# The opening of a decoder layer: c spread over partitions by TensorE, a plain second gate, and eight modulation columns computed later

## The chip, the cores and the metric

The kernel runs on one core of a Trainium2 chip. The metric is the device time of one execution in microseconds. A core has a matrix engine (TensorE, PE in the profile), which loads a stationary operand (PEld) and streams a moving one past it, and three others for elementwise work: VectorE (DVE), ScalarE (ACT) and GpSimd (POOL). SyncE (SP) issues the DMAs here. Data stands in SBUF, 128 partitions wide; matmul results stand in PSUM, in eight banks of 128 x 512 f32.

## The reference

One decoder layer on x (1024 tokens x 1024) with a condition c (one row of 1024):

```
mods = SiLU(c) @ W_ada + b_ada            # 9 rows of 1024: shift, scale, gate of 3 sub-layers
x = LN1(alpha*x + (1+g1) * 1/2 * SwiGLU_1(x*(1+sc1) + sh1))
x = LN2(alpha*x + (1+g2) * TokenMix(x*(1+sc2) + sh2))
x = LN3(alpha*x + (1+g3) * 1/2 * SwiGLU_2(x*(1+sc3) + sh3))
SwiGLU(h) = (silu(h @ w_gate) * (h @ w_up)) @ w_down      # w_gate, w_up: 1024 x 2816
```

TokenMix is two groups of attention heads between an input and an output projection; the change does not touch it. All inputs are f32.

## The kernel before

**Exact products.** Every f32 operand of a large matmul is split in a high part (ACT casts it to fp32r, line 101) and a low part (DVE subtracts, line 102). `mm3` then issues three matmuls, high x high, high x low and low x high (lines 106 to 108), into one PSUM bank.

**Modulation.** A column block of 128 modulation values is the dot product of 128 rows of the transposed W_ada (`adaT`) with SiLU(c). SiLU(c) stands as a row on every partition (`silu`, 128 x 1024). `ada_mul` (line 119) multiplies one 128 x 1024 block by it and sums along the row, on DVE; the bias comes in as the start value of the sum, and the columns of `modc` take the results. There are 72 such blocks: 16 for shift and scale of the first FFN (m = 0, 1), computed in the opening, and 56 others. `more_ada` (line 655) issues these one by one beside FFN 1: each combination step of a product calls it through `beside`, it adds 57 to a count, and whenever the count reaches 120 it takes the next block of `rest`: a DMA into ring `q` and one `ada_mul` on DVE behind that combination step.

**FFN, gate and up.** The 22 column tiles of 128 of w_gate and w_up are worked in 11 groups of two. A group's gate, and then its up part, is a 2 x 2 block product (two weight column tiles by two token halves of 512, over two halves of the 1024 rows). From group 1 on it is done with seven block products instead of eight (class `Seven`, after Winograd): each is 4 x 3 = 12 matmuls, 84 in all, against 96 for the plain form. For this, `w_ops` (line 246) combines weight blocks on DVE (lines 265 to 271) and splits seven of them; the moving side takes the blocks B11, B21, B22 of the modulated input and the combinations T1 to T4 (`t_sum`, line 219; `t_split`, line 238); and the products are combined out of PSUM on DVE (lines 306 to 327). `use_gate` then forms gate * (1 + tanh(gate/2)) and `use_up` multiplies by the up part. `a_store` writes the group's result with its own combinations to DRAM for the down projection.

**Opening.** Lines 530 to 538 load c twice, each half spread by a DMA to all 128 partitions, and form SiLU(c). `start_ffn1` (line 562) works group 0 in the plain form, in eight chunks of 128 rows of x, `d` = 0 to 7: load two blocks of adaT and one of x^T, compute the two modulation columns, modulate (ACT, line 598), split, and issue 24 matmuls into eight PSUM banks (weights `w0` and `w1`, each a gate and an up tile). From d = 4 on each chunk also forms T1 to T4 of rows d - 4 and splits T1 and T2. Then come SiLU and product of group 0 (lines 627 to 629), the weights of group 1's gate (line 630) and the splits of T3 and T4.

**FFN 2** uses the same code. Its first three pairs of products are begun early, while the second token half is still being normalized (line 1306); two of these keep their sums in ring `b` until lines 308 to 313 and 341 or 345 have read them. After that `gate_up` runs at line 1330, and `more_ada` with it (line 1329), with nothing left in `rest`.

**Buffers and order.** Tiles come from rings (line 41): `h` 14 of 8 KB per partition, `w` 6, `u` 6, `t` 7, `z` and `q` 4, `b` 2. PSUM banks have rings too: `mm` 3, `y` 2, `tp` 2, `o` 1. A tile waits until a buffer of its ring is free. The order of instructions on each engine is laid out by the framework's planner, from its own estimate of when operands and buffers are ready, and can differ from the order of the code; on the chip each engine then works its list in order.

Of the kernel before, what the change touches and what calls it, by code (L numbers as in the profile page):

```python
# [9 lines left out]
AF = mybir.ActivationFunctionType  # L10
# [4 lines left out]
P = 128  # L15
# [30 lines left out]
def layer_kernel(ctx, tc, xT, x, c, adaT, adab, wg1, wu1, wd1, wqk, wv1, wv2, bf, sinks,  # L46
# [26 lines left out]
    def psum(tag):  # L73
        return mk(ps, [P, HT], F32, tag, BANK[tag])
# [39 lines left out]

        return [st("h", [P, 4, HT], F32R) for _ in range(2)]

    silu = st("b", [P, D])

    def ada_mul(w, j):
        m = j // KD  # L120
        s = 0.125 if m in (2, 8) else 0.5
        V.tensor_tensor_reduce(w, w, silu, scale=s, scalar=bcol[:, j:j + 1], op0=ALU.mult,
                               op1=ALU.add, accum_out=modc[:, j:j + 1])

    def ada_block(m, d):
# [162 lines left out]
    class Seven:  # L288


        def __init__(self, ops, use):
            self.ops, self.use, self.n, self.wo = ops, use, 0, {}

        def run(self, order, hold=None):
            for i in order:
# [52 lines left out]
    def gate_up(wg, wu, ops, ai, g0, wo, a=None, begun=()):  # L348
        ahead = list(begun)

        def order_of(s):
            return ORDER0 if s.n else ORDER

        def go(s):
            if s.n:
                s.use(0, 0, s.c11)
            s.run(order_of(s))

        for g in range(g0, NG):
            prev = a  # L360
            a, sg, su = ahead.pop(0) if ahead else gu_pair(ops)
            sg.wo.update(wo)
            su.wo.update(w_ops(wu, 2 * g, order_of(su)))
            go(sg)
            if prev:
                a_store(ai, g - 1, prev)
            wo = w_ops(wg, 2 * g + 2, order_of(ahead[0][1]) if ahead else ORDER) if g + 1 < NG else None
            go(su)
        a_store(ai, NG - 1, a)
# [157 lines left out]
        return xs[1]  # L527


    for n in range(2):  # L530
        cs = slice(n * HT, (n + 1) * HT)
        DMA.dma_start(silu[:, cs], c[0, cs].partition_broadcast(P))
        th = st("t", [P, HT])
        A.activation(th, silu[:, cs], AF.Tanh, scale=0.5)
        V.scalar_tensor_tensor(silu[:, cs], th, 1.0, silu[:, cs], op0=ALU.add, op1=ALU.mult)
    DMA.dma_start(bcol, adab)
    for m in (1, 4, 7, 2, 5, 8):
# [24 lines left out]
    def start_ffn1():  # L562
        ops = {}
        hd = []
        blk = {}
        w0 = w1 = None
        p0 = [[psum("mm"), psum("mm")], [psum("mm"), psum("o")]]
        p1 = [[psum("y"), psum("y")], [psum("tp"), psum("tp")]]
        ada = {}

        def fetch(d):
            if d < KD:
                ada[d] = st("h", [P, 2, D])
                for m in range(2):
                    j = m * KD + d
                    DMA.dma_start(ada[d][:, m], adaT[j * P:(j + 1) * P, :])
                hd.append(st("z" if d < 4 else "q", [P, S]))
                DMA.dma_start(hd[d], xT[d * P:(d + 1) * P, :])

        def modulation(d):  # L580
            if d < KD:
                for m in range(2):
                    ada_mul(ada[d][:, m], m * KD + d)

        fetch(0)
        modulation(0)
        for d in range(KD):
            t = hd[d]
            if d:
                fetch(d + 1)  # L590
            if d in (0, SECOND):
                if d == 0:
                    w0 = [weight_std(wg1, 0, "w"), weight_std(wu1, 0, "w")]
                for _, load in w0:
                    load(d > 0)
            if d == 0:
                fetch(1)
            A.activation(t, t, AF.Identity, bias=modc[:, d:d + 1], scale=modc[:, KD + d:KD + d + 1])
# [12 lines left out]
            for w, p in ((w0, p0), (w1, p1)):  # L611
                for q in range(2):
                    for hf in range(2):
                        hi, lo = blk[d // 4, hf]
                        mm3(p[q][hf], *w[q][0][d], hi[:, d % 4], lo[:, d % 4], d == 0, d == KD - 1)
            if d >= 4:
                for n in ("T1", "T2", "T3", "T4"):
                    t_sum(n, hd, ops, d - 4, V)
                for n in ("T1", "T2"):
                    t_split(n, ops, d - 4)  # L620
        ops["B11"], ops["B21"], ops["B22"] = blk[0, 0], blk[1, 0], blk[1, 1]
        a = []
        for j, p in enumerate((p0, p1)):
            a.append(st("z", [P, S]))
            for hf in range(2):
                t = halves(a[j])[hf]
                A.activation(t, p[0][hf], AF.Tanh, scale=0.5)
                V.scalar_tensor_tensor(t, t, 1.0, p[0][hf], op0=ALU.add, op1=ALU.mult)
                V.tensor_tensor(t, t, p[1][hf], ALU.mult)
# [4 lines left out]
        return ops, wo, a  # L634

    ops1, wo1, a1 = start_ffn1()

    DMA.dma_start(ident, consts[0])
    DMA.dma_start(upper, consts[1])
# [5 lines left out]
    V.memset(ones, 1.0)  # L645
    V.memset(nhalf, -0.5)
    V.tensor_scalar(nsink, sinkb, -1.0, None, op0=ALU.mult)

    rest = [(m, d) for m in range(2, 9) for d in range(KD)]

    rows_due = []

    pace = [0, 0]

    def more_ada(after, every):


        pace[0] += every
        if pace[0] < 120:
            return  # L660
        pace[0] -= 120
        while rows_due:
            gate_store(*rows_due.pop(0))
        if rest:
            m, d = rest.pop(0)
            with tc.issue_after(after):
                ada_block(m, d)
            if d == KD - 1 and m in (2, 5, 8):
                rows_due.append(((2, 5, 8).index(m), m))
# [9 lines left out]
    last_rows()  # L679

    xpark = [dram([S, D], f"xpark{i}") for i in range(2)]

# [777 lines left out]
```

## Time and profile before

| | us |
|---|---|
| median of 3 runs | 1785.83 |
| lowest and highest | 1784.86, 1786.31 |
| the profiled execution | 1786.12 |
| its span | 1784.3 |

Of the span, PE is busy 1742.3 (98%), DVE 1511.6 (85%), ACT 781.1 (44%), POOL 23.7 (1%). Busy times of DVE and ACT count overlapping starts and ends, so operations that follow one another closely show a little more each than their distance.

A row of the timeline gives start, length, engine, line, operation, output and inputs with their shapes, how many instructions were merged, and in brackets how long the engine had been idle before it and what released it. In the views by window, each engine has its busy time and the number of instructions.

### The profile page before, as it was taken

The page shows a single profiled execution, that of the slowest core. Times are in us where ns is not written, and L with a number is a line of the kernel's source. Part 1 is how long each engine was busy: PE and PEld are TensorE (multiplying, and loading weights), DVE is VectorE, ACT ScalarE, POOL GpSimd, SP SyncE. Part 2 cuts the span into 40 slices and gives each one's busy share as a digit, 9 for nine tenths or more (in the row PEclk, how much of TensorE's full clock was granted, in tenths as well). Part 3 has the DMA queues.
Part 4 walks back from the last instruction along what each step waited for, and adds up shares of the span by engine and source line. Part 5 has one row for each costly group of instructions (what it writes and reads, how often), then busy time and mean ns, then how long its engine had stood idle before and what let it go on. Part 6 is the DMA issues. An engine that isn't in the chain of part 4 may idle for free.

```text
span 1784.3 us, 23511 instructions
## 1 busy us (share of the span) xinstructions
PE 1742.3 (98%) x8114; PEld 1438.4 (81%) x8114; DVE 1511.6 (85%) x2751; ACT 781.1 (44%) x1489; POOL 23.7 (1%) x32
## 2 busy tenths in 40 slices
PE   7999999999999999999999989999999999999997
PEld 5788888888888889877778778778888888878885
DVE  7999999999696797367887987998887887789788
ACT  5433333333444463277666652643333333344472
POOL 0000000000000000000000001000000000000000
PEclk9999999999999999999999999999999999999999
DMA  9355565556944337655678863243233232683452
GB/s 369 117 191 190 183 206 183 182 178 237 338 128 142 107 88 238 201 165 173 194 212 234 227 217 128 83 141 125 91 131 103 99 103 94 211 307 103 141 165 78
DMA packets 147047, 303.44 MB, mean 170 GB/s; under 512 B 15384, under 2 KB 29296, under 8 KB 146928
## 3 DMA queue, kind: packets, MB, share of 16 engines
q1 hardware_dynamic: 146928, 301.94, 52.4%
q8 instruction: 64, 1.05, 0.3%
q14 instruction: 55, 0.45, 0.1%
HBM read 224.17 MB, written 77.71 MB: 169 GB/s over the span
## 4 chain that ended last, share of the span: by engine, by line
PE 83%; DVE 10%; ACT 3%; DMA 2%; issue 2%; POOL 0%; SPq 0%; POOLq 0%; DVEq 0%; ACTq 0%
PE y L106 12%; PE y L108 12%; PE y L107 12%; PE mm L108 9%; PE mm L107 9%; PE mm L106 9%; PE o L106 3%; PE o L108 3%; PE o L107 3%; PE tp L108 2%; PE tp L106 2%; DVE h L102 2%; PE tp L107 2%; PE tp L1152 2%; DVE w L102 1%
## 5 line engine op out<-in xcount | busy, mean ns | idle before, releaser
L101 ACT CAST w<-u 128x512 fp32r<-128x512 f32 x295 | 181.6, 621 | 359.8 <-PE y L108 139.3
L106 PE MATMUL y<-h,w 128*128 128x512 f32 x728 | 286.6, 394 | 1.4 <-ACT w L101 1.4
L107 PE MATMUL y<-h,w 128*128 128x512 f32 x728 | 285.3, 392 | 0.0
L108 PE MATMUL y<-h,w 128*128 128x512 f32 x728 | 284.7, 392 | 0.0
L106 PE MATMUL mm<-h,w 128*128 128x512 f32 x528 | 206.9, 393 | 18.0 <-ACT h L101 15.3
L102 DVE TENSOR_TENSOR w<-u,w 128x512 fp32r<-128x512 f32 x295 | 201.6, 687 | 23.7 <-ACT w L101 22.7
L107 PE MATMUL mm<-h,w 128*128 128x512 f32 x528 | 207.4, 394 | 0.0
L108 PE MATMUL mm<-h,w 128*128 128x512 f32 x528 | 207.1, 393 | 0.1
L106 PEld LDWEIGHTS y<-h,w 128*128 128x128 f32 x728 | 136.8, 188 | 29.2 <-ACT w L101 2.4
L108 PEld LDWEIGHTS y<-h,w 128*128 128x128 f32 x728 | 136.8, 188 | 26.2
L107 PEld LDWEIGHTS y<-h,w 128*128 128x128 f32 x728 | 136.8, 188 | 25.9
L101 ACT CAST w<-t 128x512 fp32r<-128x512 f32 x106 | 65.6, 621 | 188.6 <-PE mm L108 70.6
L106 PEld LDWEIGHTS mm<-h,w 128*128 128x128 f32 x528 | 99.7, 189 | 40.0 <-ACT h L101 15.8
L108 PEld LDWEIGHTS mm<-h,w 128*128 128x128 f32 x528 | 100.3, 190 | 21.5 <-DVE w L102 1.0
L107 PEld LDWEIGHTS mm<-h,w 128*128 128x128 f32 x528 | 100.2, 190 | 21.6 <-DVE h L102 0.8
L101 ACT CAST z<-u 128x512 fp32r<-128x512 f32 x88 | 54.7, 622 | 93.8 <-PE y L108 61.3
L102 DVE TENSOR_TENSOR t<-tp,t 128x512 fp32r<-128x512 f32 (+1 forms) x126 | 72.7, 587 | 18.5 <-ACT t L101 17.3
L102 DVE TENSOR_TENSOR z<-u,z 128x512 fp32r<-128x512 f32 x88 | 60.7, 691 | 26.7 <-ACT z L101 25.3
L101 ACT CAST w<-h 128x512 fp32r<-128x512 f32 x111 | 68.3, 617 | 29.9 <-DMA h<-in_wd 11.8
L102 DVE TENSOR_TENSOR w<-h,w 128x512 fp32r<-128x512 f32 x111 | 76.2, 689 | 5.7 <-ACT w L101 5.5
L101 ACT CAST t<-tp 128x512 fp32r<-128x512 f32 (+1 forms) x126 | 62.4, 502 | 36.1 <-PE tp L1152 35.0
L102 DVE TENSOR_TENSOR w<-t,w 128x512 fp32r<-128x512 f32 x106 | 73.0, 690 | 1.6 <-ACT w L101 1.1
(349 smaller groups left out, 3917.5 us busy)
## 6 DMA issues: line engine op xcount, KB each, us to landing
u<-aT SPq DMA_DIRECT2D x154, 256.0 KB, 2.8
q<-in_adaT SPq DMA_DIRECT2D x56, 512.0 KB, 3.4
u<-in_wg SPq DMA_DIRECT2D x92, 256.0 KB, 3.2
u<-in_wu SPq DMA_DIRECT2D x90, 256.0 KB, 2.8
aT<-z SPq DMA_DIRECT2D x44, 512.0 KB, 3.2
h<-in_wd SPq DMA_DIRECT2D x88, 256.0 KB, 5.4
qkd<-w SPq DMA_DIRECT2D x26, 512.0 KB, 3.4
aT<-b SPq DMA_DIRECT2D x22, 512.0 KB, 4.3
```

Of the source, the lines that this page charges most:

```text
L101: A.copy(hi, src)
L102: V.tensor_tensor(lo, src, hi.bitcast(F32), ALU.subtract)
L106: T.matmul(o, lh, rh, start=start, stop=False, skip_group_check=more)
L107: T.matmul(o, lh, rl, start=False, stop=False, skip_group_check=more)
L108: T.matmul(o, ll, rh, start=False, stop=stop, skip_group_check=more)
L1152: T.transpose(pt[:, tok(i - q0)], sps[i][:, tok(j)], ident)
```

## The change

- c comes as one row of 4 KB on one partition (`crow`). For each half of 512 a plain f32 matmul with a row of ones as the stationary operand writes it to all partitions in PSUM (`silu_half`); tanh and product read it there.
- Of the first chunk, each dot product is done in two halves of 512, the first beside the second half of SiLU(c); the second half takes the first one's sum, with the bias added, as its start value. Scale comes before shift. The modulation of the first chunk is done by halves too.
- The two sets of four PSUM banks of group 0 are exchanged, and the order of its matmuls in a chunk goes by token half first.
- In the chunk loop only T1 is formed and split. T2 and T3 and their splits follow the loop, mixed with SiLU and product of group 0; T4 comes last.
- The gate of group 1 is done in the plain form (`direct`), with the weights `wd2` loaded and split by `weight_all` into four buffers of ring `w`; its up part stays with seven products.
- The count of `more_ada` starts at -57 x 12, and FFN 1 keeps the last eight blocks (the gate of the third sub-layer) for FFN 2, where the count goes by 20. SiLU(c) is written to DRAM as a row and spread into a buffer of ring `b` again for these.

```diff
-    silu = st("b", [P, D])
+    cond = [st("b", [P, D])]
+    silu = cond[0]
...
+        def direct(self, w, blk):
+
+            self.done = True
+            for j in range(2):
+                for hf in range(2):
+                    p = psum(BANKS[2 * j + hf])
+                    for d in range(KD):
+                        hi, lo = blk[d // 4, hf]
+                        mm3(p, *w[j][d], hi[:, d % 4], lo[:, d % 4], d == 0, d == KD - 1)
+                    self.use(j, hf, p)
...
-    for n in range(2):
+    crow = st("b", [P, D])
+    DMA.dma_start(crow[:1], c)
+    V.memset(ones, 1.0)
+
+    def silu_half(n):
+
         cs = slice(n * HT, (n + 1) * HT)
-        DMA.dma_start(silu[:, cs], c[0, cs].partition_broadcast(P))
+        pc = psum("mm")
+        T.matmul(pc, ones[:1, :], crow[:1, cs], start=True, stop=True)
         th = st("t", [P, HT])
-        A.activation(th, silu[:, cs], AF.Tanh, scale=0.5)
-        V.scalar_tensor_tensor(silu[:, cs], th, 1.0, silu[:, cs], op0=ALU.add, op1=ALU.mult)
-    DMA.dma_start(bcol, adab)
+        A.activation(th, pc, AF.Tanh, scale=0.5)
+        V.scalar_tensor_tensor(silu[:, cs], th, 1.0, pc, op0=ALU.add, op1=ALU.mult)
...
-        p0 = [[psum("mm"), psum("mm")], [psum("mm"), psum("o")]]
-        p1 = [[psum("y"), psum("y")], [psum("tp"), psum("tp")]]
+        p0 = [[psum("y"), psum("y")], [psum("tp"), psum("tp")]]
+        p1 = [[psum("mm"), psum("mm")], [psum("mm"), psum("o")]]
...
-        fetch(0)
-        modulation(0)
+        fetch(0)
+        part = small([P, 2], "part", 1)
+        for n in range(2):
+            cs = slice(n * HT, (n + 1) * HT)
+            silu_half(n)
+            for m in (1, 0):
+                w = ada[0][:, m, cs]
+                to = modc[:, m * KD:m * KD + 1] if n else part[:, m:m + 1]
+                V.tensor_tensor_reduce(w, w, silu[:, cs], scale=0.5, scalar=part[:, m:m + 1] if n else float(m),
+                                       op0=ALU.mult, op1=ALU.add, accum_out=to)
+            if n == 0:
                 for m in range(2):
+                    V.tensor_tensor(part[:, m:m + 1], part[:, m:m + 1], bcol[:, m * KD:m * KD + 1], ALU.add)
+        bias_ready(1)
...
-            A.activation(t, t, AF.Identity, bias=modc[:, d:d + 1], scale=modc[:, KD + d:KD + d + 1])
...
             for hf in range(2):
+                if d == 0 or hf == 0:
+                    y = halves(t)[hf] if d == 0 else t
+                    A.activation(y, y, AF.Identity, bias=modc[:, d:d + 1], scale=modc[:, KD + d:KD + d + 1])
...
             if d >= 4:
-                for n in ("T1", "T2", "T3", "T4"):
-                    t_sum(n, hd, ops, d - 4, V)
-                for n in ("T1", "T2"):
-                    t_split(n, ops, d - 4)
+                t_sum("T1", hd, ops, d - 4, V)
+                t_split("T1", ops, d - 4)
         ops["B11"], ops["B21"], ops["B22"] = blk[0, 0], blk[1, 0], blk[1, 1]
+        wd2 = [weight_all(wg1, c, "w") for c in (2, 3)]
+        for d in range(2):
+            t_sum("T2", hd, ops, d, V)
+            t_sum("T3", hd, ops, d, V)
+            t_split("T3", ops, d)
...
-        wo = w_ops(wg1, 2)
-        for n in ("T3", "T4"):
-            for d in range(4):
-                t_split(n, ops, d)
+        for d in range(2, 4):
+            t_sum("T2", hd, ops, d, V)
+            t_sum("T3", hd, ops, d, V)
+            t_split("T3", ops, d)
+        for d in range(4):
+            t_split("T2", ops, d)
+            t_sum("T4", hd, ops, d, V)
+        pair = gu_pair(ops)
+        pair[1].direct(wd2, blk)
+        for d in range(4):
+            t_split("T4", ops, d)
...
-    pace = [0, 0]
+    pace = [-57 * 12, 0]
...
-        if rest:
+        if len(rest) > keep:
...
-    beside.append(lambda ins: more_ada(ins, 57))
-    gate_up(wg1, wu1, ops1, 0, 1, wo1, a1)
+    beside.append(lambda ins: more_ada(ins, 57, KD))
+    gate_up(wg1, wu1, ops1, 0, 1, {}, a1, [pair1])
...
+    silu_d = dram([D], "silu_d")
+    DMA.dma_start(silu_d, silu[0])
...
-    beside.append(lambda ins: more_ada(ins, 10))
+    cond.append(st("b", [P, D]))
+    DMA.dma_start(cond[-1], silu_d.partition_broadcast(P))
+    beside.append(lambda ins: more_ada(ins, 20))
```

More of the change, by code (lines that the diff above doesn't have):

```diff
@@ L292, in __init__ @@
             self.ops, self.use, self.n, self.wo = ops, use, 0, {}
+            self.done = False
+        def direct(self, w, blk):
[7 more added lines that the diff above has]
+                    self.use(j, hf, p)
         def run(self, order, hold=None):
@@ L354, in go @@
         def go(s):
+            if s.done:
+                return
             if s.n:
@@ L573, in fetch @@
                 ada[d] = st("h", [P, 2, D])
-                for m in range(2):
+                for m in (1, 0):
                     j = m * KD + d
                     DMA.dma_start(ada[d][:, m], adaT[j * P:(j + 1) * P, :])
+                if d == 0:
+                    DMA.dma_start(bcol, adab)
                 hd.append(st("z" if d < 4 else "q", [P, S]))
@@ L611, in start_ffn1 @@
             for w, p in ((w0, p0), (w1, p1)):
-                for q in range(2):
-                    for hf in range(2):
+                for hf in range(2):
+                    for q in range(2):
                         hi, lo = blk[d // 4, hf]
@@ L628, in start_ffn1 @@
                 V.scalar_tensor_tensor(t, t, 1.0, p[0][hf], op0=ALU.add, op1=ALU.mult)
+            for hf in range(2):
+                t = halves(a[j])[hf]
                 V.tensor_tensor(t, t, p[1][hf], ALU.mult)
-        wo = w_ops(wg1, 2)
-        for n in ("T3", "T4"):
-            for d in range(4):
-                t_split(n, ops, d)
-        return ops, wo, a
-    ops1, wo1, a1 = start_ffn1()
+        for d in range(2, 4):
[9 more added lines that the diff above has]
+            t_split("T4", ops, d)
+        return ops, a, pair
+    ops1, a1, pair1 = start_ffn1()
     DMA.dma_start(ident, consts[0])
```

14 lines of the change are left out of this document (9 added, 5 removed).

## The prediction

> **What bounds the kernel now.** I read the page's busy shares and its chain first, then the busy time by windows, and then the order of events in the opening.
>
> ```profile
> PE 83%; DVE 10%; ACT 3%; DMA 2%; issue 2%; POOL 0%; SPq 0%; POOLq 0%; DVEq 0%; ACTq 0%
> ```
> ```profile
> 40.00:60.00 20.00, 17.37 (x70) 13.92 (x69) 20.00 (x35) 10.89 (x16) 0.00 (x0) 0.91 0.35 119
> 60.00:80.00 20.00, 19.18 (x84) 15.05 (x83) 19.70 (x35) 9.88 (x19) 0.00 (x0) 1.00 0.38 125
> ```
> ```profile
> 85.10:123.00 37.90, 37.90 (x168) 31.09 (x167) 37.10 (x62) 12.33 (x21) 0.00 (x0) 1.00 0.55 178
> ```
>
> The matmuls set the end (PE 83% of the chain). After the columns for start:end and length come PE, PEld, DVE, ACT, POOL, granted clock, DMA share and GB/s. From 85 on PE is full. Whatever there is to win lies before 85, and it reaches the end undiminished, since full PE follows.
>
> ```profile
> 12.72 0.80 PE L106 MATMUL mm<-h,w 128*128 128x512 f32 x1 [12.72 <-ACT h L101]
> ...
> 17.96 0.63 PE L108 MATMUL o<-h,w 128*128 128x512 f32 x1
> ...
> 21.81 0.39 PE L106 MATMUL mm<-h,w 128*128 128x512 f32 x1
> ...
> 48.78 0.39 PE L108 MATMUL tp<-h,t 128*128 128x512 f32 x1
> 51.80 0.73 PE L106 MATMUL mm<-h,w 128*128 128x512 f32 x2 [2.63 <-ACT h L101]
> ...
> 54.44 0.63 PE L107 MATMUL mm<-h,w 128*128 128x512 f32 x1
> 54.87 0.63 PE L108 MATMUL mm<-h,w 128*128 128x512 f32 x1
> ...
> 64.19 0.39 PE L108 MATMUL tp<-h,t 128*128 128x512 f32 x1
> 64.81 0.47 PE L106 MATMUL mm<-h,w 128*128 128x512 f32 x1 [0.23 <-DVE z L628]
> ...
> 66.09 0.51 PE L106 MATMUL mm<-h,w 128*128 128x512 f32 x1 [0.58 <-ACT w L101]
> ```
> ```profile
> 85.18 0.48 PE L106 MATMUL y<-h,w 128*128 128x512 f32 x1
> ```
>
> From the timeline of PE. Chunks d=1 to 5 hold 120 matmuls, 21.81 to 48.78: 26.97/119 = 0.2266 us each. Group 0 has 192, the gate of group 1 has 7 products of 12 = 84, and at 85.18 its up part begins. 12.72 + 276 x 0.2266 = 75.26, so 9.92 us are lost behind the first matmul:
> - 3.65 in d=0 (21.81 - 12.72 - 24 x 0.2266): the first twelve come at 0.43 instead of 0.23, then the second weights are late.
> - 4.53 in d=6 and 7 (64.42 - 21.81 - 168 x 0.2266): 2.63 of idling, then half rate (54.44 to 54.87).
> - 1.73 in the gate of group 1 (85.18 - 64.42 - 84 x 0.2266): three short waits for its operands.
>
> **What it changes, step by step.**
>
> *The start.*
> ```profile
> 4.12 0.63 ACT L534 ACTIVATE t<-b 128x512 f32<-128x512 f32 x1 [2.10 <-DMA b<-in_c]
> ...
> 6.23 1.29 DVE L535 SCALAR_TENSOR_TENSOR b<-t,b 128x512 f32<-128x512 f32 x2
> ...
> 7.85 1.28 DVE L122 CUSTOM_DVE_ANT_0 h<-h,b,bcol 128x1024 f32<-128x1024 f32 x1 [0.33 <-DMA h<-in_adaT]
> ...
> 10.40 1.24 ACT L598 ACTIVATE z<-z,modc 128x1024 f32<-128x1024 f32 x1 [4.32 <-DVE modc L122]
> 11.55 0.60 ACT L101 CAST w<-u 128x512 fp32r<-128x512 f32 x1
> 12.06 0.61 ACT L101 CAST h<-z 128x512 fp32r<-128x512 f32 x1
> ```
> ```profile
> 0.00:3.00 3.00, 0.00 (x0) 0.00 (x0) 0.18 (x2) 1.28 (x1) 0.20 (x4) 1.00 0.32 72
> 3.00:7.00 4.00, 0.00 (x0) 0.00 (x0) 1.21 (x8) 1.26 (x2) 0.00 (x0) 1.00 1.00 276
> 7.00:20.00 13.00, 6.93 (x17) 4.56 (x18) 9.63 (x16) 6.18 (x10) 0.00 (x0) 1.00 1.03 409
> ```
> Today c (0.52 MB after spreading) goes ahead of the 1.05 MB of adaT, and the DMA runs at 276 GB/s until 7. The dot products begin at 7.85 for want of adaT. With 4 KB in place of 0.52 MB, adaT should land near 5.9 (7.8 less 0.52 MB/276 GB/s = 1.9). The new chain: c lands about 3.2 (the 256 KB took to 4.1); TensorE spreads a half in two instructions, estimated at the cold 0.43 each with 0.2 of latency, so the halves are out at 4.3 and 5.2; tanh 0.63, product 0.69: 5.65. So the dots still wait for adaT, at 5.9. From there DVE has two half dot products at some 0.72 (half of 1.28, and a read of the sum), two tiny adds at an estimated 0.1, the second product 0.65 and two more dots: 9.63. Half the modulation (0.63) and a cast (0.61): first matmul at 10.9, that is 1.8 earlier; the weights' cast that stood at 11.55 finds idle ACT time before. Ends: 0.5 earlier (adaT no sooner than 7.2, since all transfers share the engines) and 3.2 (adaT at 5.0, two tenths less per dot, c at 2.7).
>
> No row has a plain f32 matmul of 512 columns. The nearest:
> ```profile
> L811 PE MATMUL tp<-t,upper x2: 275/288/302, 727.3 to 727.5; 128*128 128x64 f32 x2
> ```
> One call is two instructions there, which is what I took. The Trainium skill ("FP8 and Floating Point Precision", section "TensorE Precision Notes") speaks against it: true FP32 takes 4 passes through the array. By that rule each half would cost 1.7 instead of 0.86, the dots would begin at 6.4, and the kernel would give 0.5 back (1781.6 in place of the time below). The 64-column row is too short to tell.
>
> The 3.65 of d=0 I leave: the same cold clock, and the second weights come after the same work.
>
> *Only T1 in the chunk loop.*
> ```profile
> L122 DVE CUSTOM_DVE_ANT_0 h<-h,b,bcol 128x1024 f32<-128x1024 f32 x6 | 7.5, 1280 | 0.0
> ...
> L229 DVE TENSOR_TENSOR t<-q,z 128x512 f32<-128x512 f32 x4 | 2.8, 688 | 0.0
> L235 DVE TENSOR_TENSOR q<-q,t 128x512 f32<-128x512 f32 x4 | 2.8, 688 | 0.0
> ```
> ```profile
> 47.32 1.28 DVE L122 CUSTOM_DVE_ANT_0 h<-h,b,bcol 128x1024 f32<-128x1024 f32 x1
> ...
> 54.56 0.69 DVE L232 TENSOR_TENSOR z<-q,z 128x512 f32<-128x512 f32 x1
> 55.16 0.69 DVE L235 TENSOR_TENSOR q<-q,t 128x512 f32<-128x512 f32 x1
> ```
> Back to back a 128x512 operation takes 0.60 (54.56 to 55.16), a dot product about 1.2. A chunk d>=4 costs DVE now 2 dots, 2 low parts, 4 sums and 2 splits: 2.4 + 8 x 0.6 = 7.2, against 24 x 0.2266 = 5.44 of PE. So DVE falls 1.8 behind per chunk and reaches the dots of chunk 6 only at 47.32; the pause at 49 follows. Without T2 to T4: 2.4 + 4 x 0.6 = 4.8, under 5.44. Chunk 3, with four weight splits, costs 2.4 + 1.2 + 2.4 = 6.0, and chunks 1 and 2 have 1.8 to spare each. DVE no longer falls behind: the 4.53 go. Next late would be the DMA: some 14.7 MB at 409 GB/s end near 40, while d=7 is wanted at about 52. Both the idling and the half rate behind it count. The Trainium skill ("TensorE: Matmul & The Clock Gate", section "Part 1: The HAM clock gate (the "warmup" mystery)") puts the return to the slow clock after an idle window of about 3.4 us. By that rule 2.63 would not slow PE, and only 2.63 would be won (1783.0). The row of 54.44 disagrees: 0.43 after 2.63.
>
> *The plain gate.* 2 x 2 x 8 x 3 = 96 matmuls in place of 84: +12 x 0.2266 = 2.72. They need no T, so the 1.73 of waits go. New is the join: wd2 wants four buffers of ring w, all six being held by w0 and w1. w0's gate is last read 15 matmuls (3.4 us) before group 0 ends; cast, subtraction and the emptying of the first y bank (tanh, product) take about 2.5 in that time. Waiting casts stand in front of nothing else urgent on ACT. I take 0.4 (between 0 and the 1.73 of today's joint). DVE, from some 3 us before group 0's end to the up part's second product, has about 39 operations (4 low parts of wd2, 8 of SiLU and its product, 20 for the T2, T3 and T4 sums and the T2 and T3 splits, 4 for the up weights, 3 of the gate's own): 23.5 us, against 3.4 + 21.8 + 2.7 = 27.9. It fits by 4.4. The modulation's later start (12 marks) gives 5.7 dots (7 us) of room after it.
>
> *Columns moved.* FFN 1 loses eight dots and their DMAs. PE there waits for nothing (85.10 row), so I count nothing. In FFN 2 they meet this:
> ```profile
> 1168.86 0.61 PE L106 MATMUL mm<-h,w 128*128 128x512 f32 x1 [1.81 <-ACT w L101]
> ```
> ```profile
> 1171.02 0.70 DVE L313 TENSOR_TENSOR t<-y,b 128x512 f32<-128x512 f32 x1
> ...
> 1174.15 0.68 DVE L320 TENSOR_TENSOR t<-y,t 128x512 f32<-128x512 f32 x1
> ...
> 1180.16 1.29 DVE L102 TENSOR_TENSOR w<-t,w 128x512 fp32r<-128x512 f32 x2
> ...
> 1183.20 0.68 DVE L313 TENSOR_TENSOR t<-y,b 128x512 f32<-128x512 f32 x1
> ...
> 1190.24 0.68 DVE L265 TENSOR_TENSOR t<-u,u 128x512 f32<-128x512 f32 x1
> ```
> ```profile
> 1185.77 0.39 PE L106 MATMUL y<-h,w 128*128 128x512 f32 x1
> ```
> ```profile
> 1184.00:1250.00 66.00, 66.00 (x293) 54.67 (x292) 57.30 (x92) 20.48 (x35) 0.00 (x0) 1.00 0.35 121
> ```
> The row of c needs a buffer of ring b, and both are held until L313 has read them: the first at 1171.7. The fourth mark, behind which the first dot comes, is L320 at 1174.15. It may wait there for the row (some 2 us) and takes 1.2 itself; queued behind it are the up weights split at 1180.16, which PE wants at 1185.77, 4.4 after the first is done. So nothing to 1.8; I take 0.3. Later, one dot per six marks finds 8.7 us idle in 66. Its four first transfers take the ring q places of four others of the same size. The weights that SP could issue late behind the waiting row are first read at 1190.24.
>
> **Sum:** 10.9 + 3.65 + 288 x 0.2266 + 0.4 = 80.2 instead of 85.2, so -5.0, and +0.3: -4.7. The profiled execution took 1786.12 (its span is 1784.3, with 1.8 around it); less 4.7 that is 1781.4. The median of the runs, 1785.83, is 0.3 lower, so **1781.1**.
>
> **Rivals.**
> - *The pause moves to the joint.* The T work, wd2 and the up weights all fall behind one another on DVE, and PE idles long enough to lose its clock: another 4.5. Against it stand the 4.4 to spare; for it, that DVE is 37.1 busy of 37.9 afterwards. 1785.6.
> - *The start does not move.* PE's first matmul waits for xT and the weights, not c; then the 1.8 go: 1782.9. For it: the DMA share is 1.0 from 3 on. Against: ACT waited 4.32 for modc, not for xT.
> - *Slower: the row of c gets the second buffer of ring b,* free at 1183.9, with the dot queued on DVE at 1174.8 ahead of the weight splits. DVE stands some 14 us with landing (1174.8 to 1189), PE loses 14 + 1.2 - 4.4 = 10.8 and 2 of half rate: +12.8 - 5.0, 1793.6. It turns the result beyond 5 us of loss. Against: the first buffer is free 12 us sooner.
> - *Something better:* the waits of d=0 shrink too, by up to 2: 1779.1.
>
> **Chances.** Forecast 0.58 (1779.2 to 1783.0 with its bounds), pause 0.18, start 0.13, slower 0.07, better 0.04. Neither rule of the Trainium skill has a case of its own: the one's 1781.6 lies within the forecast, and the other's 1783.0 has a row against it. 0.2% is 3.6 us, about what a measurement of this kernel tells from no change. Faster, under 1782.3: most of the forecast, the better, a little of the start: 0.61. Same: the pause, most of the start, the late end of the forecast: 0.32. Slower: 0.07. The range leaves out the slower case, and some of the pause and of the better: 1778.7 to 1785.5.
>
> **What would show it.** Right: first split matmul near 10.9; no PE idle time over 1 us from there to the up gate's start near 80; DVE with idle time in chunks 4 to 7; PE full to the end of FFN 1. Wrong: a wait of PE for DVE's or ACT's w near 57 or 80; the first matmul still past 12; a DVE wait for the row of c behind the first mark in FFN 2 with PE idle after it; or time lost between 450 and 1110, where nothing is edited, by another order of the same work.

## The result and the profile after

| | median us | lowest, highest | ratio to before, 95% interval |
|---|---|---|---|
| before | 1785.34 | 1784.00, 1786.31 | |
| after | 1810.43 | 1808.33, 1812.68 | 1.0141 [1.0129, 1.0153] |

The changed kernel is 25.1 us slower; 1781.1 was forecast, in a range of 1778.7 to 1785.5. The profiled execution took 1808.33, with a span of 1806.5. These lines of its page answer to those of before:

```profile
span 1806.5 us, 23549 instructions
...
PE 1774.9 (98%) x8130; PEld 1438.4 (80%) x8130; DVE 1511.8 (84%) x2743; ACT 781.5 (43%) x1486; POOL 21.9 (1%) x32
...
PE 90%; DVE 6%; ACT 2%; issue 1%; DMA 0%; POOL 0%; SPq 0%; POOLq 0%; DVEq 0%; ACTq 0%
```

The span grew by 22.2 (from 1784.3) and PE's busy time by 32.6 (from 1742.3), with 16 instructions more. So PE does not stand idle longer: its idle time fell from 42.0 to 31.6, and its share of the chain rose from 83 to 90% while DVE's fell from 10 to 6%. The matmuls themselves take longer. The view by window, for PE alone, shows how evenly (length of the stretch, PE busy, its instructions, granted clock, DMA share, GB/s). First the kernel before:

```profile
200.00:250.00 50.00, 50.00 (x223) 1.00 0.57 193
500.00:550.00 50.00, 50.00 (x222) 1.00 0.36 98
```

And after:

```profile
200.00:250.00 50.00, 50.00 (x216) 1.00 0.55 189
500.00:550.00 50.00, 50.00 (x216) 1.00 0.40 121
```

The first stretch lies in the gate and up products of FFN 1, the second in its down projection. In both PE is full and the granted clock is 1.00, before and after, and yet 216 matmuls fit in 50 us where 222 did. The timeline of after gives the distance:

```profile
119.69 0.40 PE L106 MATMUL mm<-h,w 128*128 128x512 f32 x1
119.92 0.40 PE L107 MATMUL mm<-h,w 128*128 128x512 f32 x1
120.16 0.40 PE L108 MATMUL mm<-h,w 128*128 128x512 f32 x1
120.39 0.40 PE L106 MATMUL mm<-h,w 128*128 128x512 f32 x1
```

Three steps in 0.70: 0.2333 each, against 0.2266 before. But not every matmul is slower. The groups by form name the moving operand first and the stationary one second. Before:

```profile
L107 PE MATMUL y<-h,w 128*128 128x512 f32 x728 | 285.3, 392 | 0.0
...
L107 PE MATMUL tp<-w,z 128*128 128x512 f32 x132 | 51.4, 389 | 0.0
...
L107 PE MATMUL y<-w,w 128*128 128x512 f32 x44 | 17.1, 389 | 0.0
```

After:

```profile
L107 PE MATMUL y<-h,w 128*128 128x512 f32 x732 | 291.3, 398 | 0.5 <-DVE h L102 0.5
...
L107 PE MATMUL tp<-w,z 128*128 128x512 f32 x132 | 52.1, 395 | 0.0
...
L107 PE MATMUL y<-w,w 128*128 128x512 f32 x44 | 17.1, 389 | 0.0
```

Where moving and stationary operand come from different rings, h and w or w and z, the mean grew by 6 ns. Where both come from ring w it stayed at 389. The two pairs have 4308 and 1056 matmuls; what the change moved for them is the place of their tiles. The built program gives each ring a start address in its partition. In the kernel before all seven rings start at 32 modulo 128 bytes, and each tile is a multiple of 2048 bytes. After, the small tile `part` (8 bytes, given 32) stands between ring z and the rings t, w, u and q: b, h and z start at 32 modulo 128, the others at 64.

### The profile page after: what moved, and what is told of

It is laid out like the page before. It is cut to its first block, busy times and chain, and to the rows that moved or that the text cites. A ratio compares the mean times of both kernels' runs of the same rounds, so it can differ in the third digit from the quotient of the medians.

```text
span 1806.5 us, 23549 instructions
## 1 busy us (share of the span) xinstructions
PE 1774.9 (98%) x8130; PEld 1438.4 (80%) x8130; DVE 1511.8 (84%) x2743; ACT 781.5 (43%) x1486; POOL 21.9 (1%) x32
## 4 chain that ended last, share of the span: by engine, by line
PE 90%; DVE 6%; ACT 2%; issue 1%; DMA 0%; POOL 0%; SPq 0%; POOLq 0%; DVEq 0%; ACTq 0%
PE y L106 13%; PE y L108 13%; PE y L107 13%; PE mm L108 9%; PE mm L107 9%; PE mm L106 9%; PE o L108 3%; PE o L106 3%; PE o L107 3%; PE tp L108 2%; PE tp L106 2%; PE tp L107 2%; PE tp L1205 1%; PE o L1213 1%; DVE h L102 1%
## 5 line engine op out<-in xcount | busy, mean ns | idle before, releaser
L106 PE MATMUL y<-h,w 128*128 128x512 f32 x732 | 292.2, 399 | 7.3 <-ACT h L101 6.2
L107 PE MATMUL y<-h,w 128*128 128x512 f32 x732 | 291.3, 398 | 0.5 <-DVE h L102 0.5
L108 PE MATMUL y<-h,w 128*128 128x512 f32 x732 | 290.6, 397 | 0.0
L102 DVE TENSOR_TENSOR w<-u,w 128x512 fp32r<-128x512 f32 x294 | 200.5, 686 | 22.4 <-ACT w L101 20.9
L106 PE MATMUL mm<-h,w 128*128 128x512 f32 x516 | 204.3, 396 | 1.4 <-ACT w L101 1.4
L108 PE MATMUL mm<-h,w 128*128 128x512 f32 x516 | 204.4, 396 | 0.4 <-DVE w L102 0.4
L107 PE MATMUL mm<-h,w 128*128 128x512 f32 x516 | 204.2, 396 | 0.0
L106 PEld LDWEIGHTS mm<-h,w 128*128 128x128 f32 x516 | 96.9, 188 | 25.2 <-ACT w L101 1.8
L108 PEld LDWEIGHTS mm<-h,w 128*128 128x128 f32 x516 | 96.9, 188 | 24.3 <-DVE w L102 1.0
L107 PEld LDWEIGHTS mm<-h,w 128*128 128x128 f32 x516 | 96.9, 188 | 23.2
L102 DVE TENSOR_TENSOR z<-u,z 128x512 fp32r<-128x512 f32 x88 | 60.4, 689 | 31.3 <-ACT z L101 30.0
L101 ACT CAST w<-h 128x512 fp32r<-128x512 f32 x111 | 68.3, 617 | 30.4 <-DMA h<-in_wd 10.9
L123 DVE CUSTOM_DVE_ANT_0 q<-q,b,bcol 128x1024 f32<-128x1024 f32 x56 | 71.6, 1278 | 0.6 <-DMA b<-silu_d 0.6
```

The source lines that it names most:

```text
L101: A.copy(hi, src)
L102: V.tensor_tensor(lo, src, hi.bitcast(F32), ALU.subtract)
L106: T.matmul(o, lh, rh, start=start, stop=False, skip_group_check=more)
L107: T.matmul(o, lh, rl, start=False, stop=False, skip_group_check=more)
L108: T.matmul(o, ll, rh, start=False, stop=stop, skip_group_check=more)
L123: V.tensor_tensor_reduce(w, w, cond[-1], scale=s, scalar=bcol[:, j:j + 1], op0=ALU.mult, op1=ALU.add, accum_out=modc[:, j:j + 1])
```

## The experiments

The theory in its last form: a matmul is some 6.7 ns slower (0.2333 against 0.2266; less at 64 and 128 bytes, as the counts show) when its two operands stand in SBUF at starts that differ by something other than a multiple of 256 bytes; the change pays for the 32 bytes of `part`, and the rest of it is worth what was forecast. The rival at first: the slowness belongs to the edits themselves (more traffic, other banks, another order). The period was first taken for 64 bytes, then 128; both fell, as told below. In this table the gap is the room put between h and z on one side and w on the other, and the two counts are PE's instructions in the stretches 200 to 250 and 500 to 550.

| kernel | gap, bytes | counts | median us | ratio to before, 95% interval |
|---|---|---|---|---|
| after | 32 | 216, 216 | 1810.43 | 1.0141 [1.0129, 1.0153] |
| e1, after | 64 | 216, 221 | 1806.54 | 1.0114 [1.0099, 1.0129] |
| e5, after | 128 | 217, 217 | 1806.86 | 1.0127 [1.0113, 1.0141] |
| e9, after | 256 | 223, 223 | 1780.11 | 0.9966 [0.9954, 0.9978] |
| e10, after | 512 | 222, 222 | 1779.97 | 0.9970 [0.9960, 0.9980] |
| e3, after | 0 | 222, 222 | 1780.56 | 0.9974 [0.9965, 0.9984] |
| e2, before | 32 | 216, 216 | 1815.56 | 1.0164 [1.0149, 1.0179] |
| e4, before | 64 | 216, 220 | 1811.88 | 1.0144 [1.0129, 1.0160] |
| e6, before | 0, all moved by 32 | 223, 222 | 1784.83 | 1.0001 [0.9992, 1.0010] |

### e1 to e4: the tile `part`

**e1** makes the tile 64 bytes:

```diff
-        part = small([P, 2], "part", 1)
+        part = small([P, 16], "part", 1)
```

> The changed kernel with its new small tile (the two partial sums) made 64 bytes wide instead of 8, so that everything behind it in SBUF moves by 64 bytes and not by 32. Offset theory: a matmul whose stationary and moving operands lie 32 bytes apart modulo 64 takes 0.233 instead of 0.2266 us; here both lie at 32 modulo 64 again, so the distance between matmuls of FFN 1 goes back to 0.2266 and the time to 1778 to 1783. Rival, the work of the change itself (plain gate, other order, moved columns): the bytes don't matter, about 1810 and 0.233 stay.

**e2** puts an unused tile at the same place into the kernel before:

```diff
         fetch(0)
+        V.memset(small([P, 2], "part", 1), 0.0)
         modulation(0)
```

> The kernel before with an unused tile of 32 bytes per partition (one memset) between ring z and ring w, nothing else changed. Offset theory: its matmuls with h or z on one side and w on the other go to 0.233, those with w on both sides and with h on both stay; about 5300 of the 8114 matmul records by 6.5 ns: +30 to +35, 1815 to 1820. Rival: no layout effect, 1785 to 1786.

**e3** is the kernel after with the tile ahead of all rings, so that they all move together:

```diff
     nsink = const([P, NH], "nsink")
+    part = const([P, 2], "part")
...
         fetch(0)
-        part = small([P, 2], "part", 1)
```

> The changed kernel with the small tile of 32 bytes put ahead of all rings, so that every ring moves by 32 bytes together and all start at multiples of 64. Offset theory in its relative form (only the two operands against each other count): 1778 to 1783, as with 64 bytes. Rival, absolute form (a ring w at a multiple of 64 is slow by itself): about 1810.

**e4** is e2 with 64 bytes (`small([P, 16], ...)`).

> The kernel before with 64 unused bytes between ring z and ring w. Offset theory modulo 64: no change, 1784 to 1787. Rival, an offset that counts modulo 128 or more (the rings then lie 64 apart modulo 128): slower, up to +33.

Measured: e2 lost 30 us by a tile that nothing reads, and e3 won 30 us against after with the same instructions on the same data. That leaves nothing of these 30 us to the edits. The windows of e3:

```profile
200.00:250.00 50.00, 50.00 (x222) 1.00 0.51 175
...
500.00:550.00 50.00, 50.00 (x222) 1.00 0.35 97
```

And its groups (its lines stand one lower):

```profile
L108 PE MATMUL y<-h,w 128*128 128x512 f32 x732 | 287.2, 392 | 0.4 <-DVE h L103 0.4
...
L108 PE MATMUL tp<-w,z 128*128 128x512 f32 x132 | 51.4, 389 | 0.0
```

392 and 389 again, as in the kernel before. e1 and e4 went against the first form of the theory, by which 64 bytes would be as good as none:

```profile
200.00:250.00 50.00, 50.00 (x216) 1.00 0.55 190
...
500.00:550.00 50.00, 50.00 (x221) 1.00 0.42 123
```

That is e1: h against w is as slow as with 32 bytes, w against z nearly free. So the period is not 64. Ring w stands above both h and z; it is the stationary operand in the first stretch and the moving one in the second, so at 64 bytes it seems to matter which operand stands higher. That was not tested by itself. The cheaper second stage fits e1 and e4 lying some 4 us under after and e2.

### e5, e6, e9, e10: how far apart

**e5** makes the tile 128 bytes (two small constants are kept in it, for room):

```diff
-    nhalf = const([P, 8], "nhalf")
+    nhalf = gaincol = None
...
-    gaincol = const([P, KD], "gaincol")
...
-        part = small([P, 2], "part", 1)
+        nonlocal nhalf, gaincol
+        part = small([P, 32], "part", 1)
+        nhalf, gaincol = part[:, 16:24], part[:, 24:24 + KD]
```

> The kernel after, with the tile part grown to 128 bytes (nhalf and gaincol live in it), still between ring z and rings t, w, u, q; every ring then starts at 96 modulo 128. Theory (what counts is the distance between the starts of the two operands modulo 128 bytes): 222 instructions of the matmul per 50 us in the stretch 200 to 250, and about 1780.6 us, as e3. Rival (any tile between the rings costs, or the period is longer than 128 bytes): 216 to 221 per 50 us and 1806 to 1812 us.

```profile
200.00:250.00 50.00, 50.00 (x217) 1.00 0.54 186
...
500.00:550.00 50.00, 50.00 (x217) 1.00 0.41 119
```

217, not 222: the second form fell too, though in e5 every ring starts at 96 modulo 128. What remained was a longer period, or that any tile between the rings costs.

**e6** is the control for e3: the kernel before with an unused tile of 8 bytes ahead of all rings.

```diff
     nsink = const([P, NH], "nsink")
+    part = const([P, 2], "part")
...
         fetch(0)
+        V.memset(part, 0.0)
         modulation(0)
```

> The kernel before, with an unused tile of 8 bytes ahead of all rings, so that every ring starts at 64 modulo 128, as in e3, and not at 32. Theory (only the distance between the operands counts): 222 matmuls per 50 us and no change, 1785.2 us. Rival (64 is a better start than 32, and e3 owes its gain over the kernel before to it): faster by up to 4.7 us, 1780.6. Second rival (the start itself costs, and e3 pays for it): slower, 1787 or more.

1784.83 and counts of 223 and 222: moving all rings together does nothing, so e3's gain over the kernel before is the change's own.

**e9** is e3 with 256 bytes of constants moved from ahead of the rings to the place behind ring z; **e10** does it with 512 bytes (`cmask`). Of e9, against e3:

```diff
-    nhalf = const([P, 8], "nhalf")
+    nhalf = lnc = gaincol = None
...
-    lnc = const([P, 6, KD], "lnc")
-    gaincol = const([P, KD], "gaincol")
...
+        nonlocal nhalf, lnc, gaincol
         fetch(0)
+        nhalf = const([P, 8], "nhalf")
+        lnc = const([P, 6, KD], "lnc")
+        gaincol = const([P, KD], "gaincol")
```

> e3 with 256 bytes of constants (nhalf, lnc and gaincol) placed between ring z and ring t instead of ahead of all rings; nothing else differs, and the rings take the same room. Every ring starts at 64 modulo 128, but w stands 256 bytes off the grid of h and z modulo 512. Theory (the distance between the two operands' starts counts, modulo more than 128 bytes; unshifted tiles differ by multiples of 512): if the period is 256, 222 matmuls per 50 us between 200 and 250 and 1780.6 us; if it is 512, 216 to 221 and 1800 to 1808 us. Rival (a small tile between the rings costs whatever its size, by the order of the tiles and not by the distance): 216 and 1808 us here and in e10.

> e3 with 512 bytes of constants (cmask) placed between ring z and ring t instead of ahead of all rings. Theory (distance of the operands' starts modulo 256 or 512): the grid of 512 bytes is kept, 222 matmuls per 50 us and 1780.6 us, as e3. Rival (any tile between the rings costs): 216 and 1808 us. Second rival (the grid is that of the 2048 bytes that one operand of 512 columns takes): between 216 and 221 and 1795 us or more.

The windows of e9:

```profile
200.00:250.00 50.00, 50.00 (x223) 1.00 0.52 175
500.00:550.00 50.00, 50.00 (x223) 1.00 0.34 96
```

A tile between the rings costs nothing if it is 256 or 512 bytes. So the distance decides, and of the distances tried 0, 256 and 512 are fast and 32, 64 and 128 slow.

### e7, e8, e11, e12: the parts of the change, on e3

With the rings in line, the prediction's own steps can be read. The edits here are shown against e3. The mark that I use is the start of the first down matmul (`tp<-w,z`), behind all of FFN 1's gate and up work. In e3:

```profile
443.56 0.39 PE L107 MATMUL tp<-w,z 128*128 128x512 f32 x1
```

And before:

```profile
447.35 0.48 PE L106 MATMUL tp<-w,z 128*128 128x512 f32 x1
```

**e7** puts the sums T2 to T4 back into the chunk loop:

```diff
-                t_sum("T1", hd, ops, d - 4, V)
-                t_split("T1", ops, d - 4)
+                for n in ("T1", "T2", "T3", "T4"):
+                    t_sum(n, hd, ops, d - 4, V)
+                for n in ("T1", "T2"):
+                    t_split(n, ops, d - 4)
...
-            t_sum("T2", hd, ops, d, V)
-            t_sum("T3", hd, ops, d, V)
             t_split("T3", ops, d)
...
-        for d in range(4):
-            t_split("T2", ops, d)
-            t_sum("T4", hd, ops, d, V)
```

> e3 with all four operand sums T1 to T4 and the splits of T1 and T2 back in the chunk loop, as in the kernel before. The prediction's step (the pause of 4.53 us in chunks 6 and 7 comes from them): the pause comes back, the up gate of group 1 starts at about 86.0 instead of 81.5, and the time is 1785.1. Rival (the pause came from the order of the matmuls and the later start of the chunks as well): little or no pause, start at 81.5 to 83, time 1780.6 to 1782.

1784.15, ratio 0.9997 [0.9988, 1.0005]. Its timeline:

```profile
49.80 0.50 PE L107 MATMUL y<-h,w 128*128 128x512 f32 x1 [2.19 <-ACT h L102]
...
61.71 0.39 PE L107 MATMUL o<-h,t 128*128 128x512 f32 x1
...
64.58 0.50 PE L107 MATMUL y<-h,w 128*128 128x512 f32 x1 [2.02 <-DVE z L668]
...
448.54 0.39 PE L107 MATMUL tp<-w,z 128*128 128x512 f32 x1
```

The mark comes 4.98 later than in e3, lost at two places. In the chunks the pause is 2.19 where e3 has 1.06, with half rate behind it: the last chunk's matmuls into group 0's last bank begin 2.66 later than in e3, which had

```profile
59.05 0.39 PE L107 MATMUL o<-h,t 128*128 128x512 f32 x1
```

The other 2.3 are behind group 0, where the gate's first y bank waits for the SiLU product (L668) that DVE has queued behind the splits.

**e8** computes all 56 columns beside FFN 1, from its start on, and none in FFN 2:

```diff
-    pace = [-57 * 12, 0]
+    pace = [0, 0]
...
-    beside.append(lambda ins: more_ada(ins, 57, KD))
+    beside.append(lambda ins: more_ada(ins, 60))
...
-    silu_d = dram([D], "silu_d")
-    DMA.dma_start(silu_d, silu[0])
...
-    cond.append(st("b", [P, D]))
-    DMA.dma_start(cond[-1], silu_d.partition_broadcast(P))
-    beside.append(lambda ins: more_ada(ins, 20))
```

> e3 with all 56 modulation columns beside FFN 1 (one every 2 products from the start of group 1) and none beside FFN 2, so without the second copy of the row of c. The prediction's step (the eight dots gain nothing where they left and cost 0.3 where they went): 1780.3 us, the same within the measurement. Rival (VectorE or the q ring is short in FFN 1, and the moved columns and the later start are what keep TensorE fed): waits of the matmuls for w or t in FFN 1, 1782 to 1786.

1779.49, ratio 0.9972 [0.9962, 0.9982]: the same as e3. Where the eight columns are computed, and from when on, makes no measurable difference.

**e11** makes the gate of group 1 by seven products again:

```diff
-        wd2 = [weight_all(wg1, c, "w") for c in (2, 3)]
+        wo = w_ops(wg1, 2)
...
-        pair = gu_pair(ops)
-        pair[1].direct(wd2, blk)
         for d in range(4):
             t_split("T4", ops, d)
-        return ops, a, pair
+        return ops, a, wo
...
-    gate_up(wg1, wu1, ops1, 0, 1, {}, a1, [pair1])
+    gate_up(wg1, wu1, ops1, 0, 1, wo1, a1)
```

> e3 with the gate of group 1 as seven products again (84 matmuls and their T operands) in place of the plain 96. The prediction's step (12 matmuls more, 2.72 us, against 1.73 of waits for the products' operands and 0.4 of join): the plain gate costs 1.4, so this is 1779.2 us if the waits stay at 1.73. Rival (with T2 to T4 out of the chunk loop the seven products wait for their operands, and PE loses its clock): a pause of 4 us or more behind group 0 and 1784 us or more.

1778.35, ratio 0.9958 [0.9944, 0.9972], the fastest version of the study:

```profile
60.58 0.47 PE L107 MATMUL y<-h,w 128*128 128x512 f32 x1 [1.55 <-DVE z L668]
...
442.26 0.39 PE L107 MATMUL tp<-w,z 128*128 128x512 f32 x1
```

It has one long wait of 1.55 behind group 0, again for a y bank that DVE's SiLU product empties late, and no pause of 4. Its mark is 1.30 ahead of e3's, close to the 1.4 of the prediction's step, but as a sum of other terms. From its first matmul to the up part's the gate takes 19.12 in e11 and 21.76 in e3, 2.64 less. Of this 1.34 is lost elsewhere: chunk 1 began 0.43 later in this execution, the wait of 1.55 costs more than e3's pause of 1.06 in the chunks, which e11 has not, and the up part loses 0.5. The interval overlaps that of e3, and this is one execution of each, so the size is not firm. e8 and e11 were not tried together.

**e12** takes the opening of the kernel before (c spread by DMA, dot products of 1024 columns); the modulation of the first chunk by halves and the new order of banks and matmuls stay.

```diff
-        pc = psum("mm")
-        T.matmul(pc, ones[:1, :], crow[:1, cs], start=True, stop=True)
+        DMA.dma_start(silu[:, cs], c[0, cs].partition_broadcast(P))
...
+        modulation(0)
```

> e3 with the opening of the kernel before: c spread over the partitions by DMA (0.52 MB), the dot products of chunk 0 over 1024 columns, no matmul ahead of the first split one. The prediction's step (the new opening is worth 1.8 us): first matmul at 14.2 against 12.43 and 1782.4 us. What the traces of before and after show (12.72 and 12.39): first matmul at 12.7 and 1780.9 us, the same within the measurement.

1782.16, ratio 0.9980 [0.9970, 0.9990]; the interval overlaps e3's, so the time alone leaves it open. The first matmul came at 13.25, between the two values expected, and the mark 2.82 later than in e3:

```profile
13.25 0.80 PE L107 MATMUL y<-h,w 128*128 128x512 f32 x1 [13.25 <-ACT h L102]
...
19.45 0.62 PE L107 MATMUL mm<-h,w 128*128 128x512 f32 x1 [0.34 <-ACT w L102]
...
446.38 0.39 PE L107 MATMUL tp<-w,z 128*128 128x512 f32 x1
```

In e3:

```profile
12.43 0.80 PE L107 MATMUL y<-h,w 128*128 128x512 f32 x1 [6.33 <-ACT h L102]
...
15.97 0.60 PE L107 MATMUL y<-h,w 128*128 128x512 f32 x1
16.39 0.41 PE L108 MATMUL y<-h,w 128*128 128x512 f32 x1
```

Of the 2.82, 0.82 is the first matmul. Another 1.40 lies in d=0: chunk 1 begins 9.24 behind the first matmul in e12 and 7.84 in e3. The other 0.60 is a longer pause in chunk 6 (1.65 against 1.06).

The longer half rate (0.43) at the start of e12 does not explain the 1.40. With the old opening the thirteenth matmul, the first on the second weights, begins 6.20 or 6.21 behind the first one in all five kernels that have it. In e6 full rate came after 3.9, and PE only waited longer at this place:

```profile
19.05 0.50 PE L107 MATMUL y<-h,w 128*128 128x512 f32 x1 [1.20 <-ACT w L102]
```

Chunk 1 so begins 9.06 to 9.24 behind the first matmul with the old opening. On ACT the cast of these weights stands behind the modulation of chunk 1, which waited 3.42 for DVE's dot products there, and 1.95 in e3. With the new opening PE does not wait for the second weights, and the time to chunk 1 is 7.4 to 9.1, longer where the half rate lasts longer. So the luck is in e3, where it lasted 3.96, and not in e12. Over the 14 kernels chunk 1 begins at a median of 20.9 with the new opening and 21.9 with the old. The opening is worth about 1.0 by this, some two thirds of it in d=0.

## Why the prediction was wrong

**The step that failed** is the sum: "10.9 + 3.65 + 288 x 0.2266 + 0.4". It took the distance of 0.2266, read from the kernel before, as a property of the shape, there and in all that follows. The new tile `part` was priced as two tiny adds on DVE, and its place at nothing; and all that lies behind the up part's start was taken to go on as before ("it reaches the end undiminished"). But the 32 bytes of `part` moved the stationary operands of FFN 1 and 2 against the moving ones. The up part of group 1 began at 82.59 instead of 85.18, and from there to the end the kernel took 24.8 longer. None of the rivals has this mechanism: the one that ended on the slower side, with a chance of 0.07, was about ring b, and the dot product it speaks of waited only 0.97 for its row in e3.

Of the signs of being wrong that were named, the late first matmul came (12.39); the one that fits the loss, time lost where nothing is edited, was thought of for 450 to 1110 only and by another order of the work.

After less e3 is the price of the place: 1810.43 - 1780.56 = 29.9. Of the two profiled executions it is 1806.5 - 1778.8 = 27.7, and it can be laid out by stages. After:

```profile
82.59 0.40 PE L106 MATMUL y<-h,w 128*128 128x512 f32 x1
...
455.21 0.40 PE L106 MATMUL tp<-w,z 128*128 128x512 f32 x1
...
1118.03 0.33 PE L194 MATMUL tp<-ident,h 128*128 128x128 f32 x1 [0.42 <-DVE h L179]
```

And e3, whose 443.56 stands above:

```profile
81.50 0.39 PE L107 MATMUL y<-h,w 128*128 128x512 f32 x1
...
1101.84 0.33 PE L195 MATMUL tp<-ident,h 128*128 128x128 f32 x1 [0.49 <-DVE h L180]
```

| stage | after | e3 | more |
|---|---|---|---|
| to the up part of group 1 | 82.59 | 81.50 | 1.1 |
| rest of FFN 1's gate and up | 372.62 | 362.06 | 10.6 |
| FFN 1's down, attention | 662.82 | 658.28 | 4.5 |
| FFN 2 and the end | 688.47 | 676.96 | 11.5 |

In the second stage 362.06 / 0.2266 is 1598 places, and 1598 x 0.0067 = 10.7: the distance alone. Over the kernel 5364 matmuls by 6.7 ns would be 35.9. PE's busy time grew by 31.3 (from 1743.6 in e3), and its idle time fell by 3.6, since DVE and ACT gain room where PE was waiting for them. The 4.6 between 35.9 and 31.3 are not accounted for.

**The rest of the forecast, read in e3.** 1780.56 against 1781.1: the steps hold in sum, and not one by one. So the closeness of the two is in part luck.

- *The start* (forecast 10.9, that is 1.8 earlier) is mis-sized. The first matmul comes at 12.43 in e3 and 12.39 in after, 0.3 earlier than before; over the 14 kernels here the medians are 12.53 with the new opening and 12.85 with the old. Rows of after, from PE, DVE and ACT, tell where the 1.5 went:

```profile
2.40 3.75 PE L553 MATMUL mm<-b,ones 1*128 1x512 f32 x4 [2.40 <-DMA b<-in_c]
```
```profile
6.81 0.69 DVE L556 SCALAR_TENSOR_TENSOR b<-t,mm 128x512 f32<-128x512 f32 x1 [1.02 <-ACT t L555]
7.42 0.68 DVE L616 CUSTOM_DVE_ANT_0 h<-h,b 128x512 f32<-128x512 f32 x1
```
```profile
10.31 1.52 ACT L639 ACTIVATE z<-z,modc 128x512 f32<-128x512 f32 x2
11.74 1.12 ACT L101 CAST h<-z 128x512 fp32r<-128x512 f32 x2
```

Four instructions in 3.75 are two of 0.94 for each half, and not two of 0.43. c was there by 2.4, earlier than the 3.2 reckoned, but the second half was out only at 6.1. By the Trainium skill ("FP8 and Floating Point Precision", section "TensorE Precision Notes") true FP32 takes 4 passes; with the 0.43 of one pass at half rate that makes an estimated 1.7 for a half, and the row, with 1.9, is near it. The 64-column row was misleading, and the page's price was the better one. The late second half mattered because DVE has its product ahead of the first dot products: it stood idle for 1.02 before 6.81, though by the trace's semaphores the first block of adaT had landed at 4.9. The dot products so began at 7.42 instead of 5.9, none of them beside the second half of SiLU(c), and ended at 10.28 instead of 9.63. The other 0.8 is ACT's: it modulates both halves before the first cast, at 11.74, where one half of 0.63 was reckoned. The rival in which the start does not move has the number and not the reason: what came late was the modulation, not x^T.
- *d=0* was left at 3.65. In e3 chunk 1 begins at 20.27, and 20.27 - 12.43 - 24 x 0.2266 = 2.40. The reason given for leaving it, that the second weights come after the same work, was wrong: PE does not wait for them with the new opening (e12). What is left is the half rate, which differs by execution, so the size of 1.25 is in part luck. This unforeseen gain nearly makes up for the start.
- *Only T1 in the loop* (4.53) holds in size, 4.98 by e7, and in its cause, DVE's work. But with the other edits made, only 2.7 of it is lost in chunks 6 and 7 and the rest at the joint behind group 0. The half rate behind the pause, which the prediction counted, seems to be no loss of its own. The kernel of e6 has the code of before, the same pause, and full rate behind it (the next matmuls follow at 0.23), and then waits for DVE at the joint; its mark is 0.21 ahead of before's.

```profile
51.92 0.73 PE L107 MATMUL mm<-h,w 128*128 128x512 f32 x2 [2.65 <-ACT h L102]
...
64.54 0.47 PE L107 MATMUL mm<-h,w 128*128 128x512 f32 x1 [1.44 <-DVE z L630]
```

Nor does the pause in the chunks go to nothing. e3 keeps one of 1.06:

```profile
48.69 0.50 PE L107 MATMUL y<-h,w 128*128 128x512 f32 x1 [1.06 <-ACT h L102]
```

The planner put work of T2 back into the loop there, ahead of chunk 6: two sums (L231) before its dot products on DVE, and a cast before its own on ACT:

```profile
42.03 1.29 DVE L231 TENSOR_TENSOR t<-q,z 128x512 f32<-128x512 f32 x2
```
```profile
47.52 0.60 ACT L102 CAST h<-t 128x512 fp32r<-128x512 f32 x1
```

The prediction's 4.8 of DVE per chunk has no place for these. In e11 neither stands there, and there is no pause. Nor is there one in after, with its slower matmuls, and in e8, where chunk 1 began 1.61 later than in e3: a later PE finds the operands ready.
- *The plain gate* (+2.72, less 1.73 of waits, and 0.4 of join: a loss of 1.4) was right in sum, as far as one execution tells: e11 shows 1.30, made up of other terms. The join costs no visible wait in e3, and the rival in which the pause moves there did not come in e3; in e7 (2.02) and e11 (1.55) PE does wait at that place.
- *The up part's start* is the sum of these: forecast 80.2, in e3 81.50. The start came 1.53 later, d=0 cost 1.25 less, and 1.0 more than the 0.4 of the join was lost between, most of it in the pause.
- *The columns* (+0.3, nothing won in FFN 1) were right within what can be measured: from the up part's start to the mark it is 362.06 in e3 and 362.10 in e8. In e3 PE waits 1.8 at one place in the first part of FFN 2, as it does without the moved columns in e8 and did before (1.81).

What FFN 1 gained up to the mark is 447.35 - 443.56 = 3.8 of the 5.0 forecast. The other 0.9 that the medians show (1785.21 to 1780.56, measured side by side) is not tied to a step: the stages behind the mark vary by 1 to 2 us between executions of the same instructions (658.28, 660.05 and 660.24 for the third stage in e3, e9 and e10).

## What to carry to other kernels

A kernel that is bound by TensorE has one number, the distance of its matmuls, that multiplies with everything; look at it first in the trace of a changed kernel, and if it moved at full clock with PE full, compare the addresses of its operands before looking for waits. In this kernel a new tile in SBUF, even one of a few bytes, moved the tiles allocated behind it. Placing it ahead of all the rings cost nothing (e3, e6), and neither did 256 or 512 bytes between them (e9, e10). An engine's order is the planner's: what an edit takes out of a loop is out only when the trace shows it so. A price taken from a row of another shape (64 columns for 512) wants its other bound worked into the sum as well.

## What the runs showed of the hardware that was not expected

- Matmuls of 512 columns followed one another at 0.2266 when the starts of their operands in the partition differed by a multiple of 256 bytes, and at 0.2333 when they differed by 32 bytes; 217 instead of 222 in 50 us at 128 bytes. With 64 bytes it was slow with w above h (216) and nearly free with w above z (220 or 221), where w is the moving operand. Why is not shown: the records have no reads of SBUF. Only these distances, and only tiles of these sizes and this type, were tried.
- With the new opening the first stretch of matmuls at half rate lasted between 3.5 (e9, e10) and 6.6 (e8) in nine kernels, while the granted clock of the windows read 1.00. The Trainium skill ("TensorE: Matmul & The Clock Gate", section "Part 1: The HAM clock gate (the "warmup" mystery)") has a free-running window of about 3.4 that must pass busy before the clock rises. A start anywhere in such a window gives an estimated one to two of them, and these runs fall within that. Where nothing else holds PE up, as with the new opening, one profile carries up to some 1.5 us of luck by it.
- Whether a pause is followed by half rate differed too: it was after idle times of 2.63 (before), 2.01 (e2) and 2.19 (e7), and it was not after 2.65 (e6), 1.88 (e4) and 1.65 (e12). So the length of the pause alone did not decide it.
